# A quarter of the first MLP in two row halves of the array, another in two alternating banks, and two k tiles at once in two-product matmuls

## The chip, the cores and the metric

The kernel runs on one core of one Trainium2 chip. The metric is device time in microseconds (us) from the launch to the end on that core. The kernel before takes 1659.12 us, the median of three runs (1658.55 to 1660.34). The profiled execution, from which all rows below come, has a span of 1658.8 us from its first to its last instruction.

## The reference, cut to what matters

The model is a two-layer diffusion backbone on 256 latent tokens and 256 context tokens, 1024 features wide. Layer 0 has a convolution module as its token mixer, layer 1 a bidirectional mLSTM. After each mixer comes the MLP that the change touches:

```python
def sq_relu_mlp(u, w1, w2):
    return jnp.square(jax.nn.relu(u @ w1)) @ w2

for i in range(DEPTH):
    ...
    h = layer_norm(ALPHA * h + g2 * sq_relu_mlp(modulate(h, sh2, sc2), mlp_w1[i], mlp_w2[i]), ln2_g[i], ln2_b[i])
    if need_ctx:
        ...
        hc = layer_norm(ALPHA * hc + cg2 * sq_relu_mlp(modulate(hc, csh2, csc2), mlp_w1[i], mlp_w2[i]), ...)
```

The first MLP (layer 0) runs over 512 tokens, latent and context together, with w1 of 1024x4096 and w2 of 4096x1024. The last MLP (layer 1) runs over the 256 latent tokens only. The mLSTM makes its queries as `q = xc @ w_q`, 2048x2048, and only those of the 256 latent tokens are needed.

## The kernel before, in words

Activations lie feature by feature: a tile holds 128 features as partitions and up to 512 tokens as columns. A matmul takes 128 contraction rows of a weight (one k tile) as the stationary operand and streams the tokens past it. To keep fp32 accuracy with the fast fp32r type, each value is split in a high part (`wh`, `xh`) and a low part (`wl`, `xl`, the rest), on ACT (line 150, the cast to the high part) and DVE (line 151, the subtraction). A product of a weight and an activation is then made of three matmuls into one PSUM bank, `mm3` (lines 181, 184 and 185):

```python
        a = nc.tensor.matmul(ps, wh, xh, start=start, stop=False)
        nc.tensor.matmul(ps, wh, xl, start=False, stop=False)
        lastmm[0] = nc.tensor.matmul(ps, wl, xh, start=False, stop=stop).ins
```

Where only 256 tokens are needed, a tile holds the high parts in columns 0 to 255 and the low parts in columns 256 to 511. Then two matmuls do (`mm_any`): one of 512 columns with `wh` (line 196), which makes high times high and high times low side by side, and one of 256 columns with `wl` (line 197). `joined` adds the two halves of the bank afterwards. The queries and the w1 side of the last MLP are made so. For each k tile the 512-column matmul is followed by the 256-column one; at the last k tile of a bank the two are the other way round.

`gemm` loops over groups of 256 output columns. A group loads 1 MB of weights by SP's queue (`raw_load`, three buffers), splits them into two blocks `m` of 128x1024 (eight k tiles; `split_w`, four buffers each of `wh` and `wl`), and makes one bank of 512 columns for each `m`. `psum()` gives banks of the name `mm`, three buffers in turn; `psum("cv")` has two. With `ko=2` the first two `m` of a call are made together, three matmuls of the one bank and three of the other in turn.

The first MLP goes in four quarters `c` of the 4096 hidden features (`part(c)`). Each quarter makes eight blocks `m` of the hidden layer with w1, then multiplies by the 1024 rows of w2 that belong to them, with `ko=2`. The end of each block is `e1`: a ReLU on ACT from PSUM (line 1096), a square on DVE (line 1097), and the split into `hid` high and low (lines 150 and 151). It also calls `each1`, which in the quarters 1 and 2 advances a piece of the adaLN vectors on DVE (`AdaV.step`, line 427). Every block of w2 reads all eight `hid` tiles, one for each k tile.

The order on each engine is set when the program is built, by a list scheduler that follows the program's priorities and its own estimate of when a buffer is free. Each engine then runs its list in order.

Of the kernel before, what the change touches and what calls it, by code (L numbers as in the profile page):

```python
# [12 lines left out]
ALU = mybir.AluOpType  # L13
# [4 lines left out]
E = 2048  # L18
ET = E // P
FF = 4096  # L20
T = 512
# [50 lines left out]
def hybrid_kernel(ctx: ExitStack, tc: tile.TileContext, xT, vecs_d, wdw_d, ada0_w, ada_w, wg_d, pw1a, pw1, pw2, w1_0, w2_0,  # L72
                  w1_1, w2_1, up_x, up_z, wv, wo, bo_d, wk, wq, wqT, wdown, rows_d, out):
    nc = tc.nc
# [111 lines left out]

    lastmm = [None]

    def mm_any(ps, wh, wl, r, start, stop):


        if len(r) == 2:
            mm3(ps, wh, wl, *r, start, stop)
            return
        n = r[0].shape[-1] // 2
        todo = [lambda s_, e_: nc.tensor.matmul(ps, wh, r[0], start=s_, stop=e_),  # L196
                lambda s_, e_: nc.tensor.matmul(ps[:, :n], wl, r[0][:, :n], start=s_, stop=e_)]  # L197
        if stop:
            todo.reverse()
        todo[0](start, False)  # L200
        todo[1](False, stop)
# [14 lines left out]
    def kcol(w, kt):  # L216
        if isinstance(w[0], list):
            w, kt = (w[0][kt // 4], w[1][kt // 4]), kt % 4
        return w[0][:, kt * P:(kt + 1) * P], w[1][:, kt * P:(kt + 1) * P]

    def gemm(*a, **k):
        for _ in gemm_steps(*a, **k):
            pass

    def gemm_steps(w_ap, groups, rhs, n, epi, ko=0, pre=None, spare={}, ahead=False):

        if isinstance(rhs, dict):
            parts = [(LO, rhs[0]), (HI, rhs[1])]  # L230
        else:
            parts = [(slice(0, n), rhs)]
        kh_n = len(parts[0][1]) // 8
        groups = list(groups)
        pre = dict(pre or {})
        raws = {}

        def weights(g, kh, m):
            if (g, kh, m) not in pre:
                if (g, kh) not in raws:  # L240
                    raws[g, kh] = raw_load(w_ap[g, kh])
                pre[g, kh, m] = split_w(raws[g, kh][:, m * 1024:(m + 1) * 1024])
            return pre[g, kh, m]

        todo = [(g, kh, m) for gi, g in enumerate(groups) for kh in range(kh_n) for m in (0, 1) if 2 * gi + m >= ko]

        def prepare():
            for t in todo[:2] if ahead else ():
                weights(*t)

        if ko:
            ws, pss = [], []
            for m in range(ko):
                g = groups[m // 2]
                if m not in pre:
                    if (g, 0) not in raws:
                        raws[g, 0] = raw_load(w_ap[g, 0])
                    pre[m] = split_w(raws[g, 0][:, (m % 2) * 1024:(m % 2 + 1) * 1024])
                ws.append(pre[m])
                pss.append(psum("mm" if m < 3 else "cv")[:, :n])  # L260
            for kt in range(8):
                for m in range(ko):
                    mm_any(pss[m], *kcol(ws[m], kt), rhs[kt], kt == 0, kt == 7)
            prepare()
            for m in range(ko):
                epi(m, pss[m])
        for gi, g in enumerate(groups):
            if 2 * gi + 1 < ko:
                continue
            ms = [m for m in (0, 1) if 2 * gi + m >= ko]  # L270
            pss = {m: psum(spare.get(2 * gi + m, "mm"))[:, :n] for m in ms}
            for kh in range(kh_n):
                for m in ms:
                    w = weights(*todo.pop(0))
                    for sl, r in parts:
                        for kt in range(8):
                            mm_any(pss[m][:, sl], *kcol(w, kt), r[kh * 8 + kt], kh == 0 and kt == 0,
                                   kh == kh_n - 1 and kt == 7)
                    prepare()
                    if kh == kh_n - 1:  # L280
                        epi(gi * 2 + m, pss[m])
                    yield
# [683 lines left out]
    first, half = [], []  # L966
# [85 lines left out]
    uu = []  # L1052
# [36 lines left out]
    def mlp(w1, w2, uu, res, n, g2, feed, hmake, after, each1=None, each=None, keep=None, pre=None):  # L1089

        def part(c):
            hid = {}

            def e1(m, ps, s=None, sl=slice(0, n)):
                r, q = tmp("E")[:, :ps.shape[-1]], tmp("E")[:, :ps.shape[-1]]
                nc.scalar.activation(r, ps, AF.Relu)
                nc.vector.tensor_tensor(q, r, r, op=ALU.mult)
                if m not in hid:
                    if n == T:
                        hid[m] = hmake(F32R), hmake(F32R)  # L1100
                    else:
                        t = hmake(F32R)
                        hid[m] = t[:, :n], t[:, n:2 * n]
                split(hid[m][0][:, sl], hid[m][1][:, sl], q)
                if each1:
                    each1(c, m, s)

            groups = range(4 * c, 4 * c + 4)
            if keep and c == 0:
                gemm2(w1, groups[:3], uu, HALVES, e1, keep, ko=3)  # L1110
                gemm(w1, groups[3:], uu, n, lambda m, ps: e1(m + 6, ps))
            else:
                gemm(w1, groups, uu, n, e1, ko=0 if c else 3 + Z.pre4 if pre else 3, pre=pre if c == 0 else None)
            after(c)
# [99 lines left out]
    for f in range(0, DT, 2):  # L1214
        t = tmp("S")
# [848 lines left out]
```

## Time and profile before

| | |
|---|---|
| median of the runs | 1659.12 us |
| lowest and highest | 1658.55 and 1660.34 us |
| span of the profiled execution | 1658.8 us |
| TensorE (PE) busy | 1647.3 us, 99% of the span |
| VectorE (DVE) busy | 1042.7 us, 63% |
| ScalarE (ACT) busy | 730.4 us, 44% |
| granted TensorE clock, mean | 0.998 |
| w1 of quarter 1 of the first MLP | 310.63 to 354.15 us |
| w1 of quarter 2 of the first MLP | 399.39 to 442.91 us |
| two-product matmuls of the queries | between 911 and 1096 us |
| two-product matmuls of the last MLP | in four stretches from 1471 to 1629 us |

Matmuls are pipelined: a row of the profile gives a matmul of 512 columns a duration of 0.39 us, but the next one starts long before that has passed. What a matmul costs is read from the distance between the starts of two that follow each other, not from its duration. A matmul of plain fp32 leaves two rows, and so does its weight load.

### The profile page before, as it was taken

What the parts mean: (1) busy time and instruction counts of PE and PEld (TensorE: products, weight loads), DVE (VectorE), ACT (ScalarE), POOL (GpSimd) and SP (SyncE); (2) the same over time, 40 slices, a digit from 0 to 9 for tenths busy, and PEclk for the clock granted to TensorE, in tenths of its full rate; (3) what the DMA queues carried; (4) which work ended last, traced back from release to release, by engine and by line L of the source; (5) the groups of instructions that cost most, each with busy time, mean ns of one, the idle gap of its engine ahead of it and who ended that gap; (6) DMA issues with size and microseconds to landing.
All of it is one profiled execution on the core that took longest, in us unless ns stands there. A gap on an engine that the chain in (4) does not pass through costs nothing.

```text
span 1658.8 us, 22681 instructions
## 1 busy us (share of the span) xinstructions
PE 1647.3 (99%) x8824; PEld 1357.0 (82%) x8824; DVE 1042.7 (63%) x1875; ACT 730.4 (44%) x1174; POOL 14.3 (1%) x64
## 2 busy tenths in 40 slices
PE   9999999999999999999999999999999999999998
PEld 7665998888888998877787899888878888878887
DVE  6564895666535776762254753563489776776677
ACT  4313572232324475652133533442478654555453
POOL 0000000000000000000000000000000000000001
PEclk9999999999999999999999999999999999999999
DMA  9666223434424066557774852554466655675552
GB/s 359 229 213 239 96 71 116 163 123 147 137 102 153 1 225 204 184 194 272 282 255 145 301 179 80 178 190 151 147 227 219 212 211 202 242 283 186 178 186 93
DMA packets 80411, 305.80 MB, mean 184 GB/s; under 512 B 11854, under 2 KB 30066, under 8 KB 50352
## 3 DMA queue, kind: packets, MB, share of 16 engines
q1 hardware_dynamic: 57840, 288.06, 49.5%
q10 hardware_dynamic: 22464, 16.30, 3.0%
q8 instruction: 69, 1.13, 0.3%
q14 instruction: 38, 0.31, 0.1%
HBM read 286.47 MB, written 17.86 MB: 183 GB/s over the span
## 4 chain that ended last, share of the span: by engine, by line
PE 93%; DVE 4%; DMA 1%; ACT 1%; issue 1%; SPq 0%; DVEq 0%; ACTq 0%
PE mm L181 17%; PE mm L184 17%; PE mm L185 17%; PE mm L196 7%; PE mm L197 4%; PE mm L212 3%; PE mm L214 3%; PE mm L213 3%; PE cv L212 2%; PE fl L343 1%; PE cv L214 1%; PE cv L213 1%; DVE wl L151 1%; PE ln L181 1%; PE cv L878 1%; PE ln L184 1%
## 5 line engine op out<-in xcount | busy, mean ns | idle before, releaser
L151 DVE TENSOR_TENSOR wl<-raw,wh 128x1024 fp32r<-128x1024 f32 x344 | 418.5, 1221 | 248.1 <-ACT wh L150 246.5
L150 ACT CAST wh<-raw 128x1024 fp32r<-128x1024 f32 x344 | 358.6, 1051 | 463.3 <-PE mm L184 245.1
L184 PE MATMUL mm<-u,wh 128*128 128x512 f32 (+1 forms) x808 | 292.2, 362 | 0.2 <-DVE u L603 0.2
L181 PE MATMUL mm<-u,wh 128*128 128x512 f32 (+1 forms) x680 | 244.1, 360 | 0.0
L185 PE MATMUL mm<-u,wl 128*128 128x512 f32 (+1 forms) x680 | 241.5, 356 | 0.0
L184 PEld LDWEIGHTS mm<-u,wh 128*128 128x128 f32 x808 | 153.0, 189 | 23.3 <-issue 1.0
L181 PEld LDWEIGHTS mm<-u,wh 128*128 128x128 f32 x680 | 128.8, 190 | 24.9 <-issue 6.3
L185 PEld LDWEIGHTS mm<-u,wl 128*128 128x128 f32 x680 | 128.8, 190 | 17.9
L212 PE MATMUL mm<-wh,xl 128*128 128x512 f32 x256 | 101.2, 395 | 0.9 <-ACT wh L150 0.8
L181 PE MATMUL mm<-xm,wh 128*128 128x512 f32 x256 | 101.0, 395 | 0.0
L213 PE MATMUL mm<-wh,xl 128*128 128x512 f32 x256 | 100.0, 391 | 0.0
L185 PE MATMUL mm<-xm,wl 128*128 128x512 f32 x256 | 99.7, 389 | 0.0
L214 PE MATMUL mm<-wl,xl 128*128 128x512 f32 x256 | 99.4, 392 | 0.1
L181 PE MATMUL mm<-hid,wh 128*128 128x512 f32 (+1 forms) x256 | 93.3, 364 | 0.0
L185 PE MATMUL mm<-hid,wl 128*128 128x512 f32 (+1 forms) x256 | 92.8, 363 | 0.0
L184 PE MATMUL mm<-hid,wh 128*128 128x512 f32 (+1 forms) x256 | 92.8, 363 | 0.0
L196 PE MATMUL mm<-x,wh 128*128 128x512 f32 x232 | 81.1, 398 | 0.0
L184 PE MATMUL mm<-qq,wh 128*128 128x272 f32 x256 | 73.9, 289 | 0.0
L181 PE MATMUL mm<-qq,wh 128*128 128x272 f32 x256 | 73.5, 288 | 0.0
L185 PE MATMUL mm<-qq,wl 128*128 128x272 f32 x256 | 73.5, 288 | 0.0
L196 PE MATMUL mm<-u,wh 128*128 128x512 f32 x192 | 68.6, 399 | 0.0
L1120 DVE SCALAR_TENSOR_TENSOR x<-mm,ada,x 128x256 f32<-128x256 f32 x64 | 28.5, 479 | 62.4 <-PE mm L185 62.4
(537 smaller groups left out, 3245.2 us busy)
## 6 DMA issues: line engine op xcount, KB each, us to landing
raw<-w SPq DMA_DIRECT2D x64, 1024.0 KB, 4.8
raw<-wo SPq DMA_DIRECT2D x32, 1024.0 KB, 5.3
raw<-ada_w SPq DMA_DIRECT2D x22, 1024.0 KB, 7.3
ar<-ada_w SPq DMA_DIRECT2D x80, 256.0 KB, 4.1
raw<-wv SPq DMA_DIRECT2D x16, 1024.0 KB, 7.3
raw<-wqT SPq DMA_DIRECT2D x16, 1024.0 KB, 5.6
raw<-wq SPq DMA_DIRECT2D x16, 1024.0 KB, 6.2
raw<-wk SPq DMA_DIRECT2D x16, 1024.0 KB, 4.8
```

Source lines behind the costliest of these rows:

```text
L150: c = nc.scalar.copy(hi, src)
L151: lastsub[0] = nc.vector.tensor_tensor(lo, src, hi.bitcast(F32), op=ALU.subtract).ins
L181: a = nc.tensor.matmul(ps, wh, xh, start=start, stop=False)
L184: nc.tensor.matmul(ps, wh, xl, start=False, stop=False)
L185: lastmm[0] = nc.tensor.matmul(ps, wl, xh, start=False, stop=stop).ins
L196: todo = [lambda s_, e_: nc.tensor.matmul(ps, wh, r[0], start=s_, stop=e_), lambda s_, e_: nc.tensor.matmul(ps[:, :n], wl, r[0][:, :n], st ...
L197: lambda s_, e_: nc.tensor.matmul(ps[:, :n], wl, r[0][:, :n], start=s_, stop=e_)]
L212: nc.tensor.matmul(ps, xh, wh, start=start, stop=False)
L213: nc.tensor.matmul(ps, xl, wh, start=False, stop=False)
L214: nc.tensor.matmul(ps, xh, wl, start=False, stop=stop)
L343: a = mark_unit[0] = nc.tensor.matmul(ps[32 * j:32 * j + 32], cs[:, kt, 14 - 2 * v:46 - 2 * v], blocks[kt], start=first and kt < 4, stop=l ...
L1120: nc.vector.scalar_tensor_tensor(res[m][:, sl_], p_, g[:, m:m + 1], res[m][:, sl_], op0=ALU.mult, op1=ALU.add)
```

## The change

Three things are changed, all in how TensorE's work is cut and ordered. The arithmetic stays the same up to the order of the sums.

First, the eight w1 blocks of quarter 1 are made by `rows64`. Each matmul of 128 contraction rows becomes two of 64 rows, one in the upper and one in the lower half of the array (`tile_position` row 0 and 64). The halves accumulate in two banks, one `mm` and one `cv`, and take turns instruction by instruction. The two banks are added at the end: ACT copies the `cv` bank to SBUF (line 1160 of the changed file), DVE adds the `mm` bank to it (line 1161), and `e1` reads the sum from SBUF.

Second, the eight w1 blocks of quarter 2 are made by `turns2`: both blocks `m` of a group at once, with every matmul going to the other bank than the one before it. The two `e1` follow when the whole group is done.

Third, `gemm` calls `run`, which for two-product matmuls takes two k tiles at once: both 512-column matmuls, then both 256-column ones (and the other way round for the last pair of a bank). Three-product matmuls keep their order. The first four blocks of the last MLP are made by the `ko` part of `gemm`, which is not changed.

```diff
+    def rows64(ps, other, w, rs):
+        n = len(rs)
+        for i, (xh, xl) in enumerate(rs):
+            wh, wl = kcol(w, i)
+            for j, (a, b) in enumerate(((wh, xh), (wh, xl), (wl, xh))):
+                for q, o in ((0, ps), (64, other)):
+                    r = slice(q, q + 64)
+                    lastmm[0] = nc.tensor.matmul(o, a[r], b[r], start=i == 0 and j == 0, stop=i == n - 1 and j == 2,
+                                                 tile_position=(q, 0)).ins
+
+    def turns2(pss, ws, rs):
+        n = len(rs)
+        for i, (xh, xl) in enumerate(rs):
+            for j in range(3):
+                for ps, w in zip(pss, ws):
+                    wh, wl = kcol(w, i)
+                    a, b = ((wh, xh), (wh, xl), (wl, xh))[j]
+                    lastmm[0] = nc.tensor.matmul(ps, a, b, start=i == 0 and j == 0, stop=i == n - 1 and j == 2).ins
+
+    def run(ps, w, rs, start, stop):
+        n = len(rs)
+        if len(rs[0]) == 2:
+            for i, r in enumerate(rs):
+                mm3(ps, *kcol(w, i), *r, start and i == 0, stop and i == n - 1)
+            return
+        h = rs[0][0].shape[-1] // 2
+        for i in range(0, n, 2):
+            first, last = start and i == 0, stop and i == n - 2
+            whole = [(ps, kcol(w, k)[0], rs[k][0]) for k in (i, i + 1)]
+            half = [(ps[:, :h], kcol(w, k)[1], rs[k][0][:, :h]) for k in (i, i + 1)]
+            for j, (o, a, b) in enumerate(half + whole if last else whole + half):
+                nc.tensor.matmul(o, a, b, start=first and j == 0, stop=last and j == 3)
...
-                        for kt in range(8):
-                            mm_any(pss[m][:, sl], *kcol(w, kt), r[kh * 8 + kt], kh == 0 and kt == 0,
-                                   kh == kh_n - 1 and kt == 7)
+                        run(pss[m][:, sl], w, r[kh * 8:kh * 8 + 8], kh == 0, kh == kh_n - 1)
...
+            elif n == T and c in (1, 2):
+                for g in groups:
+                    raw = raw_load(w1[g, 0])
+                    ws = [split_w(raw[:, m * 1024:(m + 1) * 1024]) for m in range(2)]
+                    if c == 2:
+                        pss = [psum() for _ in range(2)]
+                        turns2(pss, ws, uu)
+                        for m in range(2):
+                            e1(2 * (g - 4 * c) + m, pss[m])
+                        continue
+                    for m in range(2):
+                        ps, other = psum(), psum("cv")
+                        rows64(ps, other, ws[m], uu)
+                        t = tmp("E")
+                        nc.scalar.copy(t, other)
+                        nc.vector.tensor_tensor(t, ps, t, op=ALU.add)
+                        e1(2 * (g - 4 * c) + m, t)
```

How the order on the engines changes is shown at three places. In these rows the number behind a name is the buffer's, and lines of the changed file have their own numbers: 197 is the matmul of `rows64`, 208 that of `turns2`, 223 that of `run`, 1130 the ReLU.

TensorE at the start of quarter 1, before: the three products of one k tile go to one bank.

```order
L185 MATMUL mm_2943<-hid_2710,wl_2981 128x512
L181 MATMUL mm_3014<-u_1830,wh_3018 128x512
L184 MATMUL mm_3014<-u_1831,wh_3018 128x512
L185 MATMUL mm_3014<-u_1830,wl_3019 128x512
L181 MATMUL mm_3014<-u_1838,wh_3018 128x512
```

TensorE at the same place now:

```order
L185 MATMUL mm_2943<-hid_2710,wl_2981 128x512
L197 MATMUL mm_3024<-u_1830,wh_3016 128x512
L197 MATMUL cv_3025<-u_1830,wh_3016 128x512
L197 MATMUL mm_3024<-u_1831,wh_3016 128x512
L197 MATMUL cv_3025<-u_1831,wh_3016 128x512
L197 MATMUL mm_3024<-u_1830,wl_3017 128x512
L197 MATMUL cv_3025<-u_1830,wl_3017 128x512
```

Each of the 192 matmuls of the quarter has become a pair, 384 in all, without any other matmul among them. The output is still 128 rows by 512 columns; it is the contraction that is halved.

TensorE in quarter 2, at the change from its second group to its third, now:

```order
L208 MATMUL mm_3975<-u_1886,wl_3968 128x512
L208 MATMUL mm_3976<-u_1886,wl_3972 128x512
L208 MATMUL mm_4059<-u_1830,wh_4051 128x512
L208 MATMUL mm_4059<-u_1831,wh_4051 128x512
L208 MATMUL mm_4059<-u_1830,wl_4052 128x512
L208 MATMUL mm_4059<-u_1838,wh_4051 128x512
L208 MATMUL mm_4059<-u_1839,wh_4051 128x512
L208 MATMUL mm_4060<-u_1830,wh_4055 128x512
L208 MATMUL mm_4060<-u_1831,wh_4055 128x512
```

ACT at the end of the first group of that quarter, now:

```order
L150 CAST wh_4051<-raw_4049 128x1024
L1130 ACTIVATE E_3939<-mm_3889 128x512
L150 CAST wh_4055<-raw_4049 128x1024
L1130 ACTIVATE E_3953<-mm_3890 128x512
L150 CAST hid_3943<-E_3940 128x512
```

The scheduler lets the first five matmuls of a group go to its first bank. The second bank of a group is the buffer that the first bank of the group before had, and can be written only when the ReLU has read it; on ACT that ReLU stands behind a cast of the next but one group's weights.

TensorE in the last MLP, before (the middle of a block of the w1 side):

```order
L196 MATMUL mm_13178<-x_12926,wx_13069 128x512
L197 MATMUL mm_13178<-x_12926,wx_13070 128x256
L196 MATMUL mm_13178<-x_12927,wx_13069 128x512
L197 MATMUL mm_13178<-x_12927,wx_13070 128x256
L196 MATMUL mm_13178<-x_12928,wx_13069 128x512
```

TensorE in such a block now:

```order
L223 MATMUL mm_13401<-x_13150,wx_13285 128x512
L223 MATMUL mm_13401<-x_13151,wx_13285 128x512
L223 MATMUL mm_13401<-x_13150,wx_13286 128x256
L223 MATMUL mm_13401<-x_13151,wx_13286 128x256
L223 MATMUL mm_13401<-x_13152,wx_13285 128x512
```

The same matmuls stand there, with two of a size behind each other.

## Prediction, as it was put on record

> **What bounds the kernel now.** I read the page first, then the two w1 quarters by windows, then the timeline of TensorE at the places that the change touches.
>
> ```profile
> span 1658.8 us, 22681 instructions
> PE 1647.3 (99%) x8824; PEld 1357.0 (82%) x8824; DVE 1042.7 (63%) x1875; ACT 730.4 (44%) x1174; POOL 14.3 (1%) x64
> PE 93%; DVE 4%; DMA 1%; ACT 1%; issue 1%; SPq 0%; DVEq 0%; ACTq 0%
> ```
>
> TensorE is busy for 99% of the span and makes 93% of the chain that ended last. There is next to no waiting to remove, so a gain can come only from a matmul that costs less, and a loss from one that costs more or from a new wait. The span is 1658.8 us and the median of the runs 1659.12 us, so the profiled execution stands 0.3 us below the median; I add the sum of the terms to the median. A difference under 0.2% of it, 3.3 us, is about what a measurement of this kernel can't tell from none.
>
> The price of one matmul is the distance of starts. The windows are the w1 stretches of the quarters 1 and 2 (columns: length, then busy time and count of PE, weight loads, DVE, ACT, POOL; clock; DMA share; GB/s), the timeline rows the ends of quarter 1, and a piece with 256 columns:
>
> ```profile
> 310.60:354.15 43.55, 43.55 (x194) 36.05 (x192) 29.48 (x40) 16.25 (x23) 0.00 (x0) 1.00 0.43 146
> 399.39:442.91 43.52, 43.52 (x194) 36.05 (x192) 29.43 (x40) 16.23 (x23) 0.00 (x0) 1.00 0.45 146
> ...
> 310.63 0.39 PE L181 MATMUL mm<-u,wh 128*128 128x512 f32 x1
> ...
> 353.69 0.39 PE L184 MATMUL mm<-u,wh 128*128 128x512 f32 x1
> 353.92 0.39 PE L185 MATMUL mm<-u,wl 128*128 128x512 f32 x1
> 354.15 0.39 PE L181 MATMUL mm<-hid,wh 128*128 128x512 f32 x1
> 354.37 0.39 PE L184 MATMUL mm<-hid,wh 128*128 128x512 f32 x1
> 354.60 0.39 PE L185 MATMUL mm<-hid,wl 128*128 128x512 f32 x1
> 354.83 0.39 PE L181 MATMUL mm<-hid,wh 128*128 128x512 f32 x1
> 355.05 0.39 PE L184 MATMUL mm<-hid,wh 128*128 128x512 f32 x1
> ...
> 227.79 0.28 PE L184 MATMUL mm<-u,wh 128*128 128x256 f32 x1
> ...
> 228.75 0.28 PE L181 MATMUL mm<-u,wh 128*128 128x256 f32 x1
> ```
>
> Quarter 1 has 192 matmuls of 512 columns from 310.63 to 354.15 us: 43.52 us, 226.7 ns each, at clock 1.00 and with no gap. With 256 columns, eight starts take 0.96 us, 120 ns each. The two differ by 106.7 ns for 256 columns, so 512 columns stream in 213.3 ns, and 13.3 ns of each matmul do not depend on its length. That fixed part is all that a cleverer order can win in the quarters: 192 x 13.3 = 2.6 us in each.
>
> **Quarter 1, row halves.** It removes 192 matmuls and adds 384 of 64 contraction rows. The question is whether the two halves run at the same time. No row shows fp32r in row halves; the nearest is the convolution's pair of 64 rows in plain fp32 (line 853; each matmul leaves two rows here), first TensorE, then the weight loads:
>
> ```profile
> 92.68 0.69 PE L853 MATMUL ln<-A,tab 64*128 64x512 f32 x1
> 92.69 0.69 PE L853 MATMUL mm<-A,tab 64*128 64x512 f32 x1
> 93.21 0.59 PE L853 MATMUL ln<-A,tab 64*128 64x512 f32 x1
> 93.22 0.59 PE L853 MATMUL mm<-A,tab 64*128 64x512 f32 x1
> 93.74 0.50 PE L181 MATMUL mm<-u,wh 128*128 128x512 f32 x1
> 94.07 0.40 PE L184 MATMUL mm<-u,wh 128*128 128x512 f32 x1
> ...
> 92.68 0.18 PEld L853 LDWEIGHTS ln<-A,tab 64*128 64x128 f32 x1 [0.84 <-issue]
> 92.68 0.18 PEld L853 LDWEIGHTS mm<-A,tab 64*128 64x128 f32 x1
> 92.79 0.19 PEld L853 LDWEIGHTS ln<-A,tab 64*128 64x128 f32 x1
> 92.79 0.19 PEld L853 LDWEIGHTS mm<-A,tab 64*128 64x128 f32 x1
> ...
> 94.08 0.19 PEld L185 LDWEIGHTS mm<-u,wl 128*128 128x128 f32 x1
> ```
>
> The two halves, into two banks, start 0.01 us apart, and so do their loads. The second loads are taken at 92.79, while the first matmuls stream (92.79 to 93.21, 0.42 us, twice 213.3 ns as plain fp32 has two passes to a row). So halves overlap, and a load for the same half is fetched ahead. I therefore take a pair of halves at the price of the one matmul it replaces, 226.7 ns: **0 us** over the quarter. The bounds: if the fixed part went, 213.3 ns a pair, -2.6 us; if it were paid by each of the two in turn, 240.0 ns a pair, +2.6 us; if fp32r halves don't overlap at all, 453.4 ns a pair, +43.5 us. I take 0 because the fp32 rows show nothing that the two halves pay in turn beyond 0.01 us.
>
> A change between whole array and halves costs something. The row of halves that started at 93.21 has streamed by 93.63; the next whole-array load starts only at 93.74, and counted back 0.23 us from the start at 94.07, its matmul streams from 93.84: 0.2 us lost. Entering is alike: the load at 92.68 is in the open for 0.11 us. Quarter 1 has one change in and one out: **+0.4 us**. By the order no other matmul stands inside it.
>
> The quarter also adds eight copies on ACT and eight additions on DVE. Their prices, and what they lengthen, are at the quarter's end:
>
> ```profile
> 354.12 1.05 ACT L150 CAST wh<-raw 128x1024 fp32r<-128x1024 f32 x1 [1.87 <-PE mm L184]
> 355.07 0.59 ACT L1096 ACTIVATE E<-mm 128x512 f32<-128x512 f32 x1
> ...
> 356.35 0.69 DVE L1097 TENSOR_TENSOR E<-E 128x512 f32<-128x512 f32 x1
> 357.72 0.69 DVE L151 TENSOR_TENSOR hid<-E,hid 128x512 fp32r<-128x512 f32 x1 [0.69 <-ACT hid L150]
> ```
>
> ACT copies a bank in about 0.59 us and DVE adds in about 0.69 us, both read from these rows as estimates: 8 x 0.59 = 4.7 us on ACT (16.25 becomes 21 of 43.5) and 5.5 us on DVE (29.48 becomes 35). Neither becomes the bound. What is late next is the eighth `hid` tile: now it is done at 357.72 + 0.69 = 358.41 us, 4.3 us after the quarter; then about 5.6 us after. w2 takes its first two blocks together, so its last k tile comes behind 7 x 6 matmuls, 42 x 0.2267 = 9.5 us. That is the cover, with 3.9 us to spare; without it the 1.3 us would be paid once. **0 us**.
>
> **Quarter 2, two banks in turn.** Same 192 matmuls. At the start of quarter 1's w2 the bank changes after each three, at 354.83 for one, and the distances 0.22 and 0.23 us are the same within a bank and across the change. So the bank costs nothing now and alternating wins nothing: 0 us. What it adds is a wait. The second bank of a group must have been read by the ReLU of the block before, and that ReLU stands behind a cast on ACT that is itself released by the block's last `wh` matmul. In the rows above, the cast starts 0.43 us after that matmul (353.69), the ReLU 0.95 us after the cast, for 0.59 us. In the new order the last `wh` matmul of the first bank starts four matmuls, 0.91 us, before the group's end, so the cast starts 0.48 us before the end, and the ReLU is done 1.06 us after it. The five matmuls that the scheduler put ahead cover 5 x 0.2267 = 1.13 us. The wait is 0 to 0.1 us at each of four places (three group changes and the start of w2): **+0.2 us**. Behind the waiting matmul stands all of TensorE. If a second cast came ahead of the ReLU, it would be 1.0 us each, +4 us; below nothing isn't reached, since no row shows a price for the bank.
>
> The last two `hid` tiles of this quarter now come together. The second ReLU starts behind another cast, so about 2 us after the quarter, with the square, cast and subtraction (3.3 us from the ReLU's start to 358.41 above) ready at some 5.4 us, and 6 to 7 us with DVE's own casts between: still ahead of the 9.5 us. **0 us**.
>
> **Two k tiles at once.** 480 k tiles change order: 256 of the queries and 224 of the last MLP. One stretch of eight blocks in the last MLP runs from the first row to the first row of the next work; the middle rows show a reversal, where rows of a size are merged (x2); the window counts line 196:
>
> ```profile
> 1516.09:1538.52 22.43, 21.83 (x64) 1.00 0.51 179
> ...
> 1516.09 0.39 PE L196 MATMUL mm<-x,wh 128*128 128x512 f32 x1
> ...
> 1519.25 0.39 PE L196 MATMUL mm<-x,wh 128*128 128x512 f32 x1
> ...
> 1520.30 0.40 PE L196 MATMUL mm<-x,wh 128*128 128x512 f32 x1
> ...
> 1521.24 0.40 PE L197 MATMUL mm<-x,wl 128*128 128x256 f32 x2
> 1521.48 0.63 PE L196 MATMUL mm<-x,wh 128*128 128x512 f32 x2
> ...
> 1538.63 0.59 PE L1868 MATMUL mm<-F,fold 128*128 128x512 f32 x1
> ```
>
> 64 k tiles take 1538.63 - 1516.09 = 22.54 us, 352.2 ns each. By the prices of unmixed streams it would be 226.7 + 120 = 346.7 ns. So mixing the sizes costs 5.5 ns a k tile. If only going from one size to the other costs it, the new order has about half as many goings, and wins 2.8 ns x 480 = 1.3 us. Bounds: all of it, -2.7 us; nothing, because the price lies in a load that comes behind a short matmul whatever follows, 0. Three k tiles at 1519.25 to 1520.30 cost 350 ns, which is between the two and settles neither. I take **-1.0 us**.
>
> **The sum**: 0 + 0.4 + 0 (quarter 1) + 0.2 + 0 (quarter 2) - 1.0 = -0.4 us. 1659.1 - 0.4 = **1658.7 us**, no change that can be measured.
>
> **The rivals.**
>
> *A: the halves hide each other's fixed part.* While one half changes weights, the other streams, and a pair costs 213.3 ns: -2.6 us, so 1656.1 us, and 1654.4 us if the k tiles also give their whole 2.7 us. For it: the loads of the two halves are separate instructions. Against it: each half has its own sequence of load and matmul and pays its own change, and the fixed part was there with the load fetched 0.2 us ahead. [...] 10%.
>
> *B: fp32r halves take turns.* TensorE streams one half at a time, at the price of a whole matmul, from the first pair on: +43.5 us, 1702.2 us. For it: no row shows fp32r in halves. Against it: plain fp32 does overlap, with the same partitions and banks. 9%.
>
> *C: the fixed part is paid twice in a pair*, in the one stream of instructions: +2.6 us, 1661.3 us. Against it: the 0.01 us between halves. 9%.
>
> *D: quarter 2's ReLU comes late* behind a second cast: +4 us, 1662.7 us. Against it: the list has one cast ahead. 5%.
>
> *E: the third part does not do what it says*, since the price of mixing stays: 1659.7 us. This lies in the forecast's own case.
>
> **How the numbers follow.** The forecast's case (a pair at one matmul's price, 1657.0 to 1659.9 us by the bounds of the k tiles and of the wait) has 62%, A 10, B 9, C 9, D 5, and 5 are left for what I don't see, either way. Faster than 1655.8: half of A and a little unseen, 0.08. Slower than 1662.4: B, most of D, some of C and unseen, 0.18. Same: 0.74. The range leaves B and the far ends out: 1655.5 to 1663.0 us; the forecast's own range is 1657.0 to 1660.0.
>
> **What would show it.** In the changed profile, the pairs of quarter 1 (line 197) should start 0.01 us apart and repeat each 0.227 us, and its window should stay 43.5 to 44 us; 41 us means A, 46 us C, 87 us B. Line 208 should show no idle time over 0.1 us, and quarter 2 43.5 us. The last MLP's stretch of 64 k tiles should fall from 22.54 to about 22.3 us. I am wrong if fp32r halves are not what fp32 halves are, since nothing else here is larger than 4 us.

## The result, and the profile after

The changed kernel takes 1668.13 us (median of three runs, 1667.03 to 1668.48), the kernel before 1659.12 us: a ratio of 1.005 with a 95% interval of 1.003 to 1.0069. It is slower by 9 us, half a per cent. The prediction was 1658.7 us and its range ended at 1663.0. The profiled execution has a span of 1666.3 us, 7.5 us more than before. First the span's row and the engines of its page:

```profile
span 1666.3 us, 23078 instructions
PE 1648.3 (99%) x9016; PEld 1357.5 (81%) x9016; DVE 1047.9 (63%) x1883; ACT 734.8 (44%) x1182; POOL 14.3 (1%) x64
```

Nothing in these two rows tells where 7.5 us went: TensorE is busy for 99% as before. The windows of the changed stretches tell it (columns: length, then busy time and count of PE, weight loads, DVE, ACT, POOL; clock; DMA share; GB/s): quarter 1, quarter 2, one stretch of 64 k tiles of the last MLP, and below them a piece of quarter 1 alone.

```profile
309.39:363.11 53.72, 47.24 (x386) 39.17 (x385) 34.58 (x47) 20.14 (x30) 0.00 (x0) 0.94 0.36 118
408.50:452.42 43.92, 43.92 (x194) 35.81 (x193) 26.58 (x37) 14.14 (x20) 0.00 (x0) 1.00 0.42 144
1523.93:1546.36 22.43, 22.43 (x130) 19.63 (x128) 17.74 (x29) 13.12 (x22) 0.00 (x0) 1.00 0.51 179
...
344.40:349.20 4.80, 4.77 (x24) 3.81 (x26) 3.17 (x5) 2.66 (x4) 0.00 (x0) 0.52 0.59 215
```

Quarter 1 takes 53.7 us instead of 43.5, 10.2 us more; TensorE is idle there for 6.5 us, and for some 5 us it runs at a clock of 0.52. Quarter 2 takes 43.9 instead of 43.5, 0.4 more. A stretch of 64 k tiles takes 22.43 us instead of 22.54. By the distances of starts the span adds up as follows: quarter 1 +10.2, quarter 2 +0.4, the queries -0.6, the last MLP to the end -0.4, the stretch between the queries and the last MLP -1.1 (TensorE stood still there for 0.8 us before the change, until 1409.98, and doesn't now), the two stretches around quarter 2 +0.3 together, and -1.2 because quarter 1 began 1.2 us earlier. That last term has nothing to do with the change: the kernel before has 3.41 us at half clock from 60.42 us on, ahead of everything that the change touches, where the changed kernel has full clock (0.50 and 1.00 from 60.42 to 63.8 us); and of ten profiles of this study five, that of the kernel before among them, begin quarter 1 at 310.6 to 310.9 us and five, that of the change among them, at 309.0 to 309.4, with and without row halves on both sides. So the sums below are counted from the start of quarter 1.

How the row halves run is seen in TensorE's timeline at the start of quarter 1, and then at the three places where it stands still:

```profile
309.07 0.39 PE L185 MATMUL mm<-hid,wl 128*128 128x512 f32 x1
309.39 0.49 PE L197 MATMUL mm<-u,wh 64*128 64x512 f32 x1
309.40 0.49 PE L197 MATMUL cv<-u,wh 64*128 64x512 f32 x1
309.73 0.39 PE L197 MATMUL mm<-u,wh 64*128 64x512 f32 x1
309.73 0.39 PE L197 MATMUL cv<-u,wh 64*128 64x512 f32 x1
309.96 0.39 PE L197 MATMUL mm<-u,wl 64*128 64x512 f32 x1
309.97 0.39 PE L197 MATMUL cv<-u,wl 64*128 64x512 f32 x1
...
331.31 0.39 PE L197 MATMUL mm<-u,wh 64*128 64x512 f32 x1
333.37 0.49 PE L197 MATMUL cv<-u,wh 64*128 64x512 f32 x1 [1.68 <-ACT E L1160]
...
338.73 0.39 PE L197 MATMUL cv<-u,wl 64*128 64x512 f32 x1
340.96 0.50 PE L197 MATMUL mm<-u,wh 64*128 64x512 f32 x1 [1.84 <-DVE E L1161]
344.43 0.79 PE L197 MATMUL cv<-u,wh 64*128 64x512 f32 x1 [2.97 <-ACT E L1160]
344.43 0.79 PE L197 MATMUL mm<-u,wh 64*128 64x512 f32 x1
345.02 0.62 PE L197 MATMUL cv<-u,wh 64*128 64x512 f32 x1
345.02 0.62 PE L197 MATMUL mm<-u,wl 64*128 64x512 f32 x1
345.44 0.62 PE L197 MATMUL cv<-u,wl 64*128 64x512 f32 x1
```

The two halves of a pair start within 0.01 us of each other and a pair follows the last after 0.23 us. Up to 331 us quarter 1 loses nothing but the 0.1 us of the first step. Then TensorE waits three times for a bank: 1.68 us for a copy of line 1160, 1.84 us for an addition of line 1161, 2.97 us for another copy. Behind the last one a pair takes 0.43 us, twice 512 columns' 213.3 ns, for about ten pairs, which costs 2.2 us. The stalls also put the halves out of step: four matmuls run alone (331.31, 338.73, 340.96 and the last one, 362.79), so that 192 pairs take 194 steps, 0.45 us more. The three stalls with their restarts cost 7.2 us (from the distances of starts), half clock 2.2, the two extra steps 0.45, and the two changes between whole array and halves 0.2 inside the quarter: 10.1 of the 10.2 us.

Why the banks come free late is told by the waits of all engines from 309 to 364 us (in total, times, longest), and by the timelines of ACT and then DVE:

```profile
ACT E L1130 <- DVE E L1161: 21.9, 7, 7.6
...
DVE L L461 <- DMA ar<-ada_w: 4.8, 2, 3.1
...
PE cv L197 <- ACT E L1160: 4.6, 2, 3.0
...
PE mm L197 <- DVE E L1161: 1.8, 1, 1.8
```

```profile
321.42 0.58 ACT L1160 COPY E<-cv 128x512 f32<-128x512 f32 x1
329.20 0.63 ACT L1130 ACTIVATE E<-E 128x512 f32<-128x512 f32 x1 [7.21 <-DVE E L1161]
331.27 0.62 ACT L150 CAST hid<-E 128x512 fp32r<-128x512 f32 x1 [1.43 <-DVE E L1131]
331.79 1.04 ACT L150 CAST wh<-raw 128x1024 fp32r<-128x1024 f32 x1
332.74 0.58 ACT L1160 COPY E<-cv 128x512 f32<-128x512 f32 x1
...
320.57 0.88 DVE L457 TENSOR_SCALAR L<-ar,cs 128x512 f32<-128x512 f32 x2
321.36 1.41 DVE L461 SCALAR_TENSOR_TENSOR L<-ar,cs,L 128x512 f32<-128x512 f32 x2
324.47 2.96 DVE L461 SCALAR_TENSOR_TENSOR L<-ar,cs,L 128x512 f32<-128x512 f32 x4 [1.71 <-DMA ar<-ada_w]
327.35 1.22 DVE L151 TENSOR_TENSOR wl<-raw,wh 128x1024 fp32r<-128x1024 f32 x1
328.49 0.68 DVE L1161 TENSOR_TENSOR E<-mm,E 128x512 f32<-128x512 f32 x1
...
336.43 2.74 DVE L461 SCALAR_TENSOR_TENSOR L<-ar,cs,L 128x512 f32<-128x512 f32 x4 [3.07 <-DMA ar<-ada_w]
```

Read it from below. Between the first addition and the second, VectorE's list now holds four adaLN steps (lines 457 and 461, two instructions each). They need pieces of `ada_w` that come through two buffers, and wait for them, 1.71 us here and 3.07 us before the third addition. So the second addition comes at 328.49, though its block was done on TensorE, and its `cv` bank copied, at 322. ScalarE's ReLU, which before the change read the bank by itself, now needs the addition's result and waits 7.21 us; behind it in ScalarE's list stand the cast of `hid`, a cast of weights and the copy that frees the next `cv` bank, which starts at 332.74. That copy's end, 333.32, is what TensorE waits for until 333.37. ScalarE kept the order of its list here: the copy at 332.74 came behind the ReLU that waited, though its own block had been done on TensorE at 325.9.

Three causes are possible: the **order** that the scheduler gave VectorE's list; the new **dependency** of ScalarE on VectorE, which would cost in any order; or the **row halves** on the array itself. And within the order: the steps' own work, or their waits for transfers.

### The profile page after: what moved, and what is told of

It is laid out like the page before. It is cut to its first block, busy times and chain, and to the rows that moved or that the text cites. A ratio compares the mean times of both kernels' runs of the same rounds, so it can differ in the third digit from the quotient of the medians.

```text
span 1666.3 us, 23078 instructions
## 1 busy us (share of the span) xinstructions
PE 1648.3 (99%) x9016; PEld 1357.5 (81%) x9016; DVE 1047.9 (63%) x1883; ACT 734.8 (44%) x1182; POOL 14.3 (1%) x64
## 4 chain that ended last, share of the span: by engine, by line
PE 93%; DVE 3%; DMA 1%; ACT 1%; issue 1%; SPq 0%; DVEq 0%; ACTq 0%
PE mm L181 16%; PE mm L184 15%; PE mm L185 15%; PE mm L223 10%; PE mm L248 4%; PE mm L250 4%; PE mm L249 4%; PE mm L208 3%; PE cv L248 1%; PE fl L377 1%; PE cv L250 1%; PE cv L249 1%; PE cv L197 1%; PE ln L181 1%; PE cv L912 1%; PE ln L184 1%
## 5 line engine op out<-in xcount | busy, mean ns | idle before, releaser
L184 PE MATMUL mm<-u,wh 128*128 128x512 f32 (+1 forms) x680 | 241.7, 356 | 0.2 <-DVE u L637 0.2
L181 PE MATMUL mm<-u,wh 128*128 128x512 f32 (+1 forms) x552 | 193.7, 352 | 0.0
L185 PE MATMUL mm<-u,wl 128*128 128x512 f32 (+1 forms) x552 | 191.1, 347 | 0.0
L184 PEld LDWEIGHTS mm<-u,wh 128*128 128x128 f32 x680 | 128.6, 189 | 18.1 <-issue 1.0
L181 PEld LDWEIGHTS mm<-u,wh 128*128 128x128 f32 x552 | 104.4, 189 | 19.7 <-issue 5.9
L185 PEld LDWEIGHTS mm<-u,wl 128*128 128x128 f32 x552 | 104.4, 189 | 13.0
L1294 DVE SCALAR_TENSOR_TENSOR E<-pad,vecs,E 128x512 f32<-128x512 f32 x64 | 47.9, 749 | 24.8 <-ACT E L1292 23.6
L181 PEld LDWEIGHTS mm<-xm,wh 128*128 128x128 f32 x256 | 48.0, 188 | 18.2 <-issue 5.0
```

The lines of the kernel that those rows point to most:

```text
L1294: nc.vector.scalar_tensor_tensor(s2_(acc), pad[:, :, k:k + C], V("w_conv", m * QTAP + k), s2_(acc), op0=ALU.mult, op1=ALU.add)
```

## Experiments

In all of them "quarter 1" is the time from its first matmul to the first of its w2 side in the profiled execution; it is 43.5 us before and 53.7 us with the change. All ratios are to the kernel before on the same chip.

**Which part of the change it is.** First quarter 1 alone, then everything but quarter 1:

```diff
# quarter 1 alone: the kernel before, with
+            elif n == T and c == 1:
...
+                        rows64(ps, other, ws[m], uu)
+                        t = tmp("E")
+                        nc.scalar.copy(t, other)
+                        nc.vector.tensor_tensor(t, ps, t, op=ALU.add)
+                        e1(2 * (g - 4 * c) + m, t)
# all but quarter 1: the changed kernel, with
-            elif n == T and c in (1, 2):
+            elif n == T and c == 2:
```

> The kernel before with quarter 1 of the first MLP in row halves, and nothing else of the change. All theories: if quarter 1 alone carries the loss, quarter 1 takes 53 to 54 us instead of 43.5 and the kernel 1668 to 1669.5 us (ratio 1.0055 to 1.006). Against it: if part of the loss comes from the two other parts (quarter 2, the two k tiles at once), it stays under 1667.

> The changed kernel with quarter 1 as it was before: quarter 2 in turns and two k tiles at once are left. By the two traces these are worth +0.4 us in quarter 2 and -0.6 to -1.5 us in the queries and the last MLP: 1658 to 1659 us, ratio 0.9993 to 1.0. If the loss came from them, 1660 or more.

Quarter 1 alone: 1667.88 us, ratio 1.0046 (1.0034 to 1.0059), quarter 1 54.2 us. All but quarter 1: 1659.6 us, ratio 0.9996 (0.9987 to 1.0005), quarter 1 43.5 us. The whole loss lies in quarter 1. Both times missed their expectations by a little: 1667.88 was to be 1668 at least if quarter 1 carried it all, and 1659.6 lies between the 1658 to 1659 of the one theory and the 1660 of the other; the lengths of quarter 1 decide.

**Order, dependency or halves.** One kernel keeps the whole change but doesn't let an adaLN step stand ahead of the subtraction that ends its block (`lastsub`; `issue_after` puts an instruction behind another one in its engine's list). The other does what quarter 1 now does, copy, addition and dependency, but on the whole array:

```diff
# steps held back: the changed kernel, with
-        if c in (1, 2) or (c == 3 and m < 2):
+        if c == 1:
+            with tc.issue_after(lastsub[0]):
+                ada_n1.step()
+        elif c == 2 or (c == 3 and m < 2):
             ada_n1.step()
# sum of two banks: the kernel before, with
+                        ps, other = psum(), psum("cv")
+                        for kt in range(8):
+                            mm3(ps if kt < 4 else other, *kcol(ws[m], kt), *uu[kt], kt % 4 == 0, kt % 4 == 3)
+                        t = tmp("E")
+                        nc.scalar.copy(t, other)
+                        nc.vector.tensor_tensor(t, ps, t, op=ALU.add)
```

> The changed kernel, but in quarter 1 an adaLN step may not stand ahead of the subtraction that ends its block's hid tile, so that the steps are spread one to a block on VectorE. Order theory (the additions come late because up to four steps with their waits for ada_w stand ahead of them): quarter 1 falls from 53.7 to 43.6 to 45 us, the waits of L197 on the banks go, the kernel takes 1658 to 1660 us. Dependency theory (ScalarE's ReLU now waits for VectorE, whatever the order): quarter 1 stays above 50 us, the kernel above 1665.

> The kernel before with quarter 1 on the whole array, but its first four k tiles summed in one bank and its last four in another, with the same copy and the same addition behind them as the change has: everything of the change's quarter 1 but the row halves. In the list of VectorE one adaLN step stands between two additions, not three or four. Order theory: quarter 1 takes 43.5 to 45 us, the kernel 1659 to 1660.5. Dependency theory: quarter 1 takes over 50 us, the kernel over 1665. If it is the halves on the array itself that cost, quarter 1 takes 43.5 us.

With the steps held back, quarter 1 takes 43.8 us and the kernel 1657.94 us, ratio 0.9988 (0.9980 to 0.9997). With the sum of two banks on the whole array quarter 1 takes 43.5 us and the kernel 1659.27 us, ratio 0.9999 (0.9990 to 1.0008). The windows of quarter 1 in the two, in this order:

```profile
309.33:353.01 43.68, 43.68 (x384) 35.81 (x384) 30.13 (x41) 19.41 (x28) 0.00 (x0) 1.00 0.40 133
```

```profile
309.10:352.62 43.52, 43.52 (x194) 36.05 (x193) 33.45 (x47) 20.23 (x30) 0.00 (x0) 1.00 0.42 146
```

384 matmuls in row halves in 43.68 us, at clock 1.00 and with no idle time: the halves by themselves cost nothing. Only the place of the adaLN steps was changed, and the loss is gone: the order theory stands. The dependency by itself costs nothing as long as the addition is on time. (In the second kernel's trace two steps stand ahead of the second addition and one and a half to two between later ones, not the one that was expected.) The same place in VectorE's and ScalarE's timelines of the kernel with the steps held back:

```profile
320.42 0.87 DVE L457 TENSOR_SCALAR L<-ar,cs 128x512 f32<-128x512 f32 x2
321.41 1.23 DVE L151 TENSOR_TENSOR wl<-raw,wh 128x1024 fp32r<-128x1024 f32 x1
322.55 0.68 DVE L1161 TENSOR_TENSOR E<-mm,E 128x512 f32<-128x512 f32 x1
...
323.27 0.63 ACT L1130 ACTIVATE E<-E 128x512 f32<-128x512 f32 x1 [1.41 <-DVE E L1161]
```

The ReLU waits for the addition here too, but for 1.41 us instead of 7.21, and nothing comes of it. ScalarE's list is word for word that of the change in this stretch.

Why the scheduler bunches the steps was only argued: with twice as many matmuls to a block it may take a block for twice as long, and put more of the steps between two additions. What speaks for it is that the sum of two banks, with 24 matmuls to a block as before, has at most two steps between two additions, and the change four. The scheduler's own prices were not read.

**The steps' work or their waits.** In the next kernel the bunched steps read a tile that lies in SBUF anyway, and eight loads of 256 KB are left out:

```diff
# quarter 1 in row halves alone, and in AdaV.load
+            if fake[0] is not None:
+                self.i += 1
+                return fake[0]
...
+            fake[0] = hold[0] if c == 1 else None   # hold[0] is uu[0][0]
             ada_n1.step()
```

> The kernel before with quarter 1 in row halves, and in quarter 1 the adaLN steps read a tile of u instead of newly loaded pieces of ada_w (so the adaLN numbers of the second layer are wrong and 8 loads of 256 KB are left out). The steps still stand bunched ahead of the additions, five of them (ten instructions of 0.7 us) before the second addition, but none waits for a transfer. If it is the waits for ada_w that make the additions late, quarter 1 falls to 44 to 46 us and the kernel to 1659 to 1661 us. If the steps' own work is enough (10 x 0.7 us ahead of one addition, with 5.44 us for a block), quarter 1 stays at 48 us or more, the kernel at 1663 or more.

1661.57 us, ratio 1.0008 (0.9998 to 1.0017), quarter 1 46.1 us. Its waits from 305 to 364 us:

```profile
ACT E L1112 <- DVE E L1137: 17.9, 8, 7.2
...
PE cv L197 <- ACT E L1136: 1.5, 1, 1.5
```

The expectation for the waits was 44 to 46 us and 1659 to 1661, and both came out just above the upper end. The bunch still makes one ReLU wait 7.2 us, and TensorE stands still once, for 1.5 us, at full clock afterwards (1.00 from 330 to 350 us). So of the 10.6 us that quarter 1 in row halves loses, about 2.5 come from the work of the bunched steps alone and about 8 only with their waits for `ada_w`. The split is rough: eleven instructions of the steps stand ahead of the second addition here, and eight in the change, and the transfers that are left out no longer run beside the loads of w1. The waits seem to feed on themselves, as SyncE's queue of the change shows:

```profile
328.60 0.33 SPq L144 DMA_DIRECT2D raw<-w  x1
330.66 8.87 SPq L470 DMA_DIRECT2D ar<-ada_w  x4
```

The 1 MB load of w1 at 328.60 was held until the subtraction that frees its buffer, 327.35 + 1.22 = 328.57, which stands behind the steps on VectorE. The next pieces of `ada_w` are issued behind it, the first at 330.66, when the step at 329.22 gave back one of the two buffers; four go out over 8.9 us, one for each buffer that comes free. The first landed 5.7 us after its issue, where the median of the eight is 3.2; it ran beside that 1 MB load, which is the likely reason, though no run separates it. VectorE waits for it until 336.43.

**Is it ScalarE's ReLU that matters, or any wait?** Here ReLU and square are one instruction on VectorE, so ScalarE no longer waits at the ReLU:

```diff
# quarter 1 in row halves alone, and in e1 for its blocks
-                nc.scalar.activation(r, ps, AF.Relu)
-                nc.vector.tensor_tensor(q, r, r, op=ALU.mult)
+                nc.vector.scalar_tensor_tensor(q, ps, 0.0, ps, op0=ALU.max, op1=ALU.mult)
```

> The kernel before with quarter 1 in row halves, but ReLU and square of the sum are one instruction on VectorE, max(t, 0) times t, so that ScalarE waits for VectorE only at the last cast of a hid tile and no longer at the ReLU. The adaLN steps stand bunched as in the change. If the ReLU that waits on ScalarE, with the copies of the cv banks queued behind it, is what lets TensorE run out of banks, the waits of L197 on the copy shrink and quarter 1 falls to 44 to 48 us. The cast of hid still waits for VectorE, though: if any wait of ScalarE on the late additions is as bad, quarter 1 stays at 52 us or more and the kernel at 1667 to 1669.

1666.85 us, ratio 1.0040 (1.0027 to 1.0053), quarter 1 51.8 us. The wait has moved to the cast of `hid`:

```profile
ACT hid L150 <- DVE E L1108: 27.6, 7, 8.7
...
PE cv L197 <- ACT E L1134: 2.9, 2, 2.3
...
PE mm L197 <- DVE E L1135: 2.2, 1, 2.2
```

My first picture, in which the ReLU was the culprit, falls by this: the cast of `hid`, which waits for the same late chain, does nearly the same. Taking the ReLU away won 2.3 us of 10.6, so that the 51.8 us lie just under the 52 that were expected if any such wait is as bad.

**The same order without row halves.** If order is the cause, the loss must come back on the whole array. Three kernels take the sum of two banks, which costs nothing, and force the steps together: first with three steps ahead of the second addition and five between it and the third (the expectation says two ahead of the second; the trace has three), then with four and four, then with four and four and each copy of a `cv` bank behind the cast of the block before, as the change has it (`laststep` is the last instruction of the steps so far, `hidcast` the cast of a block's `hid`):

```diff
# the sum of two banks, with
+        if c == 1:
+            for _ in range({0: 3, 1: 5}.get(m, 0)):      # then {0: 4, 1: 4}
+                ada_n1.step()
...
+                        with tc.issue_after(hidcast[k]) if k >= 0 else nullcontext():   # the third kernel alone
+                            nc.scalar.copy(t, other)
+                        with tc.issue_after(laststep[0]) if 2 * (g - 4 * c) + m in (1, 2) else nullcontext():
+                            nc.vector.tensor_tensor(t, ps, t, op=ALU.add)
```

> Quarter 1 on the whole array with the sum of two banks (as in sum_whole, which costs nothing), but the adaLN steps put into VectorE's list in a bunch as the change's list has them, with no row halves: two steps ahead of the second addition, five ahead of the third, none behind the fifth. Order theory: the loss comes back without any row halves: TensorE waits for the banks of blocks 3 to 6, quarter 1 takes 50 to 55 us and the kernel 1665 to 1670. If the row halves have a part in the loss beside the order (their banks filling in another way, or the pairs' price), quarter 1 stays under 46 us and the kernel under 1662.

> As bunch, but with the very order of the change on VectorE: four adaLN steps ahead of the second addition and four between it and the third; still on the whole array, with no row halves. Order theory: with the later second addition TensorE waits more than in bunch, where quarter 1 took 48.8 us: 51 to 55 us, the kernel 1665 to 1669. If the row halves have a part of their own beside the order, quarter 1 stays at 46 to 50 us as in bunch, the kernel at 1661 to 1664.

> As bunch4, and on ScalarE each copy of a cv bank is held behind the cast of the block before, as the change's list has it (in bunch4 the copies of later blocks stood ahead of it, and no cv bank was waited for). Still no row halves. Theory that the loss is made by both lists together, late additions on VectorE and copies queued behind the ReLU that waits for them on ScalarE: now TensorE waits for cv banks too, and quarter 1 takes 51 to 55 us instead of 47.5, the kernel 1665 to 1669. If the copies' place does not matter, and the rest of the loss needs the row halves, quarter 1 stays at 46 to 49 us, the kernel at 1661 to 1664.

Measured: 1663.09 us, ratio 1.0018 (1.0009 to 1.0028), quarter 1 48.6 us; 1662.09 us, 1.0016 (1.0006 to 1.0025), 47.3 us; 1662.9 us, 1.0018 (1.0009 to 1.0027), 47.4 us. The loss comes back without row halves, but at most half of it, and all three sizes that the order theory gave were missed; the second and the third lie where the expectations had put row halves with a part of their own. The place of the copies, the last idea, makes no difference on the whole array. The waits of the third kernel show what is smaller:

```profile
ACT E L1098 <- DVE E L1127: 6.9, 6, 1.5
...
PE mm L181 <- DVE E L1127: 2.0, 1, 2.0
DVE L L429 <- DMA ar<-ada_w: 1.7, 4, 0.5
```

VectorE waits 1.7 us for `ada_w` here, and 4.8 us in the change; the ReLU 1.5 us at the longest, and 7.6 in the change. SyncE's list is not the same (its loads of w1 and `ada_w` alternate in another way), and ScalarE has weights to cast ahead of the ReLU, and casts them. The loss of quarter 1 goes roughly, though not strictly, with VectorE's waits for `ada_w` through the bunched kernels: 2.5 us with no wait, 3.8 and 3.9 with 1.6 and 1.7 us of waits, 5.1 with 3.4, 8.3 (ReLU and square in one) with 5.1, 10.2 (the change) with 4.8, and 10.6 with 5.4 us. That fits the order theory, but the full 10 us were not made without row halves.

The traces point at what the three kernels lack. A block in row halves writes both its banks from the first pair on. The sum of two banks writes its `cv` bank from the 13th matmul on, 12 x 0.2267 = 2.7 us later, and none of its kernels waited for a `cv` bank, while two of the change's three stalls are for one. In the change the fifth block was due 21.9 us after the start of quarter 1, and the copy that it waited for ended at 23.9; in the third bunched kernel the same block first writes `cv` at 24.5, so that even a copy as late as that would have cost nothing. So row halves cost nothing when the banks are there, and seem to add to the loss when they aren't, by needing two at once and by running out of step; how much of the 10.2 us that is, no run separates.

**The two k tiles.** Alone, and eight k tiles in place of two. In the last MLP the eight come out as one matmul of 512 columns, eight of 256 and seven of 512:

```diff
# the kernel before, with run as in the change; or with
+        whole = [(ps, kcol(w, k)[0], rs[k][0]) for k in range(n)]
+        half = [(ps[:, :h], kcol(w, k)[1], rs[k][0][:, :h]) for k in range(n)]
+        seq = whole[:1] + half + whole[1:] if start and stop else half + whole if stop else whole + half
```

> The kernel before with two k tiles at once in the queries and the last MLP and nothing else: quarters 1 and 2 as before. By the trace of the kernel with quarter 2 in turns and two k tiles at once (from the start of quarter 1 to the end 0.6 us shorter, with 0.4 lost in quarter 2) the two k tiles alone gain 1.0 us: 1658 to 1659 us, ratio 0.9990 to 0.9996. If quarter 2's turns cost nothing when alone, no difference to that kernel is seen.

> The kernel before with eight k tiles at once, not two, in the high-low products of the queries and of the last MLP: eight matmuls of 512 columns, then eight of 256 (or the other way about in the last group), nothing else changed. If going from one size to the other is what a k tile pays for (352.2 against 346.7 ns), 7 of 8 such steps go: the 64 k tiles of a stretch fall from 22.54 to 22.2 us and the kernel by 2 to 2.6 us (1657.2 to 1657.8). If a matmul of 512 columns takes 233 ns beside any other with its own weights, as the pairs of the change suggest (350.5), the kernel gains 0.5 to 1.5 us and no more than the change's two k tiles at once.

Two at once: 1658.32 us, ratio 0.9991 (0.9982 to 1.0). Eight at once: 1658.08 us, ratio 0.9990 (0.9981 to 0.9999). The timeline of a stretch with eight at once, where rows of a size are merged:

```profile
1559.80 0.39 PE L201 MATMUL mm<-x,wh 128*128 128x512 f32 x1
1560.03 1.12 PE L201 MATMUL mm<-x,wl 128*128 128x256 f32 x8
1560.98 2.00 PE L201 MATMUL mm<-x,wh 128*128 128x512 f32 x8
1562.82 1.11 PE L201 MATMUL mm<-x,wl 128*128 128x256 f32 x8
...
1582.15 0.39 PE L226 MATMUL ln<-wh,hid 128*128 128x512 f32 x1
```

64 k tiles take 1582.15 - 1559.80 = 22.35 us, 349.2 ns each; two at once takes 350.5 and one at a time 352.2. Eight 256s in a row cost (1560.98 - 1560.03) / 8 = 119 ns, as in an unmixed stream, but eight 512s in a row (1562.82 - 1560.98) / 8 = 230 ns, not the 226.7 of the quarters. Neither theory holds as a whole. A stretch goes from one size to the other 112 times before the change, 48 times with two at once and 16 times with eight. 64 goings gone win 1.7 ns a k tile, 96 gone win 3.0, so all 112 would be worth 3.0 to 3.5 ns, out of the 5.5 by which a k tile stood above unmixed streams. The rest stays, because a 512 of this kind costs more than 226.7 ns even beside its own kind. Why was not found.

No run was made with a third buffer for the pieces of `ada_w`, so this remedy is untested.

## Why the prediction was wrong

**The step that failed** is the 0 us for the eight copies and additions of quarter 1: "ACT copies a bank in about 0.59 us and DVE adds in about 0.69 us [...] Neither becomes the bound." The prices were right (0.58 and 0.68 us), and neither engine's sum became the bound: with the steps held back ACT is busy for 19.4 and DVE for 30.1 of 43.7 us. But I priced only how much work they add, not where it stands. Ahead of the additions stood the bunched steps; behind the ReLU, the copies that free banks. As "what is late next" I named the eighth `hid` tile at the quarter's end, and priced it against 9.5 us of cover; what came late was the second addition, at 328.49, 8 us after its block, and the cover that it used up was free banks. It measured +10.2 us. VectorE's list of quarter 1 was there to be read, and I read ScalarE's list for quarter 2 alone.

The closing sentence, that nothing but unlike halves could cost over 4 us, was the same error told as a bound. The rivals A to D all sat on TensorE or in quarter 2, and none had quarter 1's epilogue as its place; 5% were left for what I didn't see.

**Row halves at the price of one matmul, 0 us: right.** A pair takes 0.227 us in fp32r as the plain fp32 rows had suggested. That plain fp32 has two passes to a row was my reading of their 0.42 us, twice 213.3 ns; no run counts passes. Rivals A (213.3 ns), B (453.4) and C (240) are refuted by the window of 384 matmuls in 43.68 us.

**Two changes between whole array and halves, +0.4 us: right.** The distances at the way in are 0.32 and 0.34 us (309.07 to 309.39 to 309.73) in place of 0.227, and with the steps held back they are the same at the way out (0.32 and 0.34): 4 x 0.1 us.

**Quarter 2, +0.2 us: right in kind, 0.4 in size.** The bank costs nothing (six matmuls from 422.21 to 423.57 us, inside a group, take 0.227 us each); the waits are those of the weight loads for the ReLU:

```profile
PEld mm L208 <- ACT E L1130: 0.8, 3, 0.3
```

There are three, 0.3 us at the longest, where up to 0.1 us each was forecast; rival D (+4 us) did not come. The last two `hid` tiles cost nothing.

**Two k tiles at once, -1.0 us: right in size.** Alone it is 1.4 us by the medians, with an interval that reaches zero, and 1.1 us by the profiles from quarter 1 to the end. The reason given, that only going from one size to the other costs, holds for 3.0 to 3.5 of the 5.5 ns, as eight at once showed.

Without the failed step the sum would have been near: with the steps held back the profile is 1.1 us shorter from quarter 1 to the end than that of the kernel before, where -0.4 was forecast.

## What to carry to other kernels

An added instruction has a place as well as a price. Before a sum of busy times is called harmless, read the list of its engine: what stands ahead of it, what that waits for, and which buffers are freed only behind it. And when an edit changes the number of instructions on one engine, look at what a scheduler did to the lists of the others; here the part that was meant (row halves) did what was expected, and a side effect on work that has nothing to do with it brought a loss of 10 us.

Two cheap tests told most: pinning the order while keeping the change, and making the same chain without the change's main part.

## What the hardware showed

- Row halves need not stay in step. After the first stall a pair is the `cv` half of one matmul with the `mm` half of the next (the rows at 345.02), and still costs one matmul, 0.227 us at full clock. What is lost is the step in which a half runs alone.
- Around a stall TensorE ran at half clock. In the changed kernel the granted clock is 0.50 from 342.20 to 349.03 us, and behind the 2.97 us wait, which ends at 344.43, about ten pairs take 0.427 us each. That is twice 213.3 ns: the 13.3 ns that a matmul costs beyond its columns at full clock (an estimate from 226.7 ns for 512 columns and 120 ns for 256) are not seen at half. In these traces half clock comes in pieces of 3.41 us: one before the change (60.42 to 63.84 us), two in a row with it (6.83 us), and about 3.4 us in each bunched kernel on the whole array (mean clock 0.83 from 340 to 350 us in the first two; 0.95 from 330 to 340 and 0.88 from 340 to 350 in the third). By the clock records of the two traces it begins 54.61 us (16 x 3.413, before) and 337.92 us (99 x 3.413, with the change) after their first record of full clock. In the 3.41 us ahead of it TensorE had been idle, by the profile, for 1.92 us (56%) in the second bunched kernel and 1.99 us (58%) in the third, in a single wait each. A wait of 1.95 us in quarter 1 in row halves alone was not followed by half clock (1.00 from 330 to 340 us). Before the change, the idle time in the 3.41 us ahead of 60.42 is one wait of 0.46 us, at 58.32; the changed kernel has that wait too, at 58.63, and full clock behind it. So the length of a wait alone doesn't tell whether half clock follows, and what does was not shown. Where it follows, a stall costs more than its idle time: 3.4 us idle in the first of the three bunched kernels cost 5.1 us.
- A matmul of 512 columns costs 226.7 ns in the quarters and, in the two-product stream of the last MLP, 231 ns (eight of a size behind each other), 232 (two) or 235 (one at a time) on average, at the same granted clock (1.00) and with no idle time; the 256s beside it cost 117 to 120 in all three orders.
